# Two transformer blocks on one core: modulation sums in PSUM tiles of their own, another order of work in the opening, and the memory's projections placed differently

## The chip, the core and the metric

The kernel runs on one core of a Trainium2 chip. The metric is the device time of one execution in microseconds (us), from the median of several executions; less is better. Engine names are those of the profile: PE (TensorE, matrix products; PEld are its weight loads), DVE (VectorE), ACT (ScalarE), POOL (GpSimd), SP (SyncE, which here only issues DMAs). SPq and ACTq are the instructions with which SP and ACT issue DMAs. All arithmetic is in 32-bit floats; most products are made of a high and a low part of each operand, so that one logical product is three matmuls (high by high, high by low, low by high).

## The reference, cut to what matters

```python
# first block (x: 512 x 1024, c: 1024)
mod = silu(c) @ w_ada + b_ada                      # 3072 wide
shift, scale, gate = split(mod, 3)
h = rms_norm(x, g_pre) * (1 + scale) + shift
proj = h @ w_in                                    # q, k, v, forget gate, gates, for two attentions
...                                                # forgetting attention and sliding-window attention
x = x + gate * rms_norm(concat(oa, ob) @ w_out, g_post)
# second block (mem: 256 x 1024)
h = rms_norm_2(x, norm_g)
mem_h = rms_norm_2(mem, mem_norm_g)
...                                                # convolution, differential attention
k, v = split(mem_h @ w_mem_kv, 2)                  # 1024 columns of keys, 1024 of values
k = rms_norm_2(k.reshape(M, 4 heads, 256), kn_g)
...                                                # cross attention to the memory, gated sum, w_out
```

## The kernel before

The program is one long list of tiles and operations. An engine executes its instructions in the order in which they stand. That order is written out by hand in the opening (the engines are wrapped there in `Ordered`, whose helper is line 345, so that nearly all of the opening carries the line L345 in a profile). After the opening a scheduler sets the order from its own estimate of durations. PSUM has four pools: `mm` (three banks), `sc` (two), `tp` (two), `pv` (one). A new tile of a pool takes over the bank of the tile that many places earlier and has to wait until that one's readers are done. A tile is tracked as a whole: a write waits for earlier reads of any column of it.

**Opening, about 0 to 105 us.** SP loads the memory `mt`, the first 512 columns of the memory's weights `rawm`, the input `xn`, and the modulation weights `ada` in eight chunks of 1 MB through five buffers; chunk k yields 128 columns of shift and 128 of scale. Memory's transpose `mT` and its first key half `kb_` are made on PE. `squares` (ACT) sums the squares of x, `rsqrt_small` is ten short DVE steps, then x is scaled (two quarters on DVE, two on ACT) and `x_transpose` turns it with PE and copies it out with ACT into `xt`. The modulation sums of chunks 0, 1, 3, 4 and 6 are made by `products` (two products on ACT, six on DVE and an add) followed by `sums` (a matmul with one column of ones); those of chunks 2, 5 and 7 by `sums_pe` (matmuls with one column each). All eight write columns of one tile, `pm`. `modulate(k)` (DVE) turns two columns of `pm` into shift and scale, `hidden(k, ...)` makes the high part `hh` (ACT) and low part `hl` of the modulated input. Then come the products with `w1c` (keys, values and forget gates of the second attention; four banks `wb`, one of them of the pool `mm`), whose weights are split into `wh` (ACT cast) and `wl` (subtraction on DVE or POOL) by `load_w`; `on_pool` names the pieces that POOL gets. Weight loads use three buffers `raw`. The queries `qb` follow (96 matmuls of line L221, banks of `mm`), then the first gate `zb0` (line L202).

**Middle, about 315 to 410 us.** The first block's output product `w_out` runs in two halves of 256 rows (`hf`), each in two column halves (`cp`) of 48 matmuls. After each half comes a chain of DVE and ACT steps: a norm, the residual `yg`, its squares (ACT L961), a second norm, `hn` (DVE L924). PE transposes `hn` later, in `finish`. In between, `mem_p(i)` makes a quarter of the memory's keys and values from the stored `mT`: 48 matmuls into two `sc` banks, which ACT then copies out as `mv` (L905). Quarter 0 is the `kb_` of the opening, quarter 1 the second key half, 2 and 3 the values.

```python
for i in ((1, 2), (3,))[hf]:
    run(mem_p(i, sc_tile))
```

Of the kernel before, what the change touches and what calls it, by code (L numbers as in the profile page):

```python
# [15 lines left out]
ALU = mybir.AluOpType  # L16
# [4 lines left out]
P = 128  # L21
S = 512
NT = 4
KT = 8
# [68 lines left out]
def two_block_kernel(ctx: ExitStack, tc: tile.TileContext, A: dict, out: bass.AP):  # L93
    nc = tc.nc
    pe, act, dve, pool = nc.tensor, nc.scalar, nc.vector, nc.gpsimd
# [18 lines left out]
    def V(name, i=None):  # L114
        a, b = VEC[name]
        return vec[:, a:b] if i is None else vec[:, a + i:a + i + 1]
# [5 lines left out]
    ident, ones = C("ident"), C("ones")  # L122
# [6 lines left out]
    def f(ap):  # L129
        return ap.bitcast(F32)  # L130
# [15 lines left out]
    def mm_tile():  # L146
        return psm.tile([P, 512], F32, tag="mm", name="mm")
# [4 lines left out]
    def tp_tile():  # L152
        return pst.tile([P, 512], F32, tag="tp", name="tp")
# [176 lines left out]
    cs = const.tile([P, 8], F32, name="cs")  # L330
# [33 lines left out]
    with ExitStack() as st:  # L364
# [9 lines left out]
        mod = pa1.tile([P, 16], F32, name="mod")  # L374
        free = (pe, act, dve, pool)
        pe, act, dve, pool, sp = (Ordered(e) for e in free + (nc.sync,))
# [16 lines left out]
        def squares(x, ss, ts):  # L393
            for t in ts:
                act.activation(out=xt[:, 2 * t:2 * t + 2, :].rearrange("p a b -> p (a b)"), in_=x[:, t, :], func=AF.Square, accum_out=ss[:, t:t + 1])
# [13 lines left out]
                    dve.scalar_tensor_tensor(out=d[i % 2], in0=a[:, i, :], scalar=cs[:, i:i + 1], in1=d[i % 2], op0=ALU.mult, op1=ALU.add)  # L409
                dve.tensor_tensor(out=d[0], in0=d[0], in1=d[1], op=ALU.add)  # L410

        pm = tp_tile()

        def sums(k):
            for j in range(2):
                pe.matmul(out=pm[:, 2 * k + j:2 * k + j + 1], lhsT=accs[k][0][:, j * P:(j + 1) * P], rhs=ones[:, 0:1], start=True, stop=True)

        def sums_pe(k):
            for j in range(2):
                for i in range(KT):  # L420
                    pe.matmul(out=pm[:, 2 * k + j:2 * k + j + 1], lhsT=adas[k][:, i, j * P:(j + 1) * P], rhs=cs[:, i:i + 1], start=(i == 0), stop=(i == KT - 1))

        def modulate(k):
            c_ = slice(2 * k, 2 * k + 2)
            dve.scalar_tensor_tensor(out=mod[:, c_], in0=pm[:, c_], scalar=0.5, in1=V("b_ada")[:, c_], op0=ALU.mult, op1=ALU.add)
            dve.scalar_tensor_tensor(out=gs[:, k:k + 1], in0=mod[:, 2 * k + 1:2 * k + 2], scalar=1.0, in1=V("g_pre", k), op0=ALU.add, op1=ALU.mult)

        def hidden(k, by, eng):
# [34 lines left out]
        xss = pa.tile([P, NT], F32, tag="xss", name="xss", bufs=1)  # L463
        squares(mt, mss, range(2))
        dve.tensor_copy(out=mrs, in_=rsqrt_small(pa, mss, 2, 1.0 / 1024, 1e-6, "rn2"))
        squares(xn, xss, range(NT))
        r = rsqrt_small(pa, xss, NT, 1.0 / 1024, 1e-6, "rn4")
        products(0, act)
        for t in range(2):
            dve.tensor_scalar(out=xn[:, t, :], in0=xn[:, t, :], scalar1=r[:, t:t + 1], scalar2=None, op0=ALU.mult)  # L470
            act.activation(out=xn[:, t + 2, :], in_=xn[:, t + 2, :], func=AF.Copy, scale=r[:, t + 2:t + 3])
        products(0, dve)
        products(1, act)
        products(1, dve)
        x_transpose(range(KT))
        sums(0)
        sums_pe(2)
        load_ada(5, 6, 7)
        sums(1)
        products(3, act)  # L480
        modulate(0)
        hidden(0, dve, pool)
        for t in range(2):
            act.activation(out=mk[:, t, :], in_=kb_[t], func=AF.Copy, scale=mrs[:, t:t + 1])
        products(3, dve)
        modulate(1)
        hidden(1, dve, pool)
        products(4, act)
        products(4, dve)
        modulate(2)  # L490
        hidden(2, dve, pool)
        sums_pe(5)
        sums(3)
        sums_pe(7)
        sums(4)
        products(6, act)
        modulate(5)
        hidden(5, act, pool)
        modulate(3)
        hidden(3, act, pool)  # L500
        w = load_w(A["w1c"], 264, on_pool=(1, 3), queue=sp)
        sp.dma_start(out=mT_d, in_=mT)
        products(6, dve)
        modulate(7)
        hidden(7, act, pool)
# [386 lines left out]
    def mem_p(i, bank):  # L892

        if not MV:
            mh, ml = (mvp.tile([P, KT, 256], F32R, name=n) for n in ("mh", "ml"))
            nc.sync.dma_start(out=f(ml), in_=mT_d)
            act.copy(out=mh, in_=f(ml))
            pool.tensor_tensor(out=ml, in0=f(ml), in1=f(mh), op=ALU.subtract)
            MV[0] = (mh, ml)
        w = load_w(A["w_mem"][i], NW)  # L900
        banks = [bank() for t in range(2)]
        yield from mm_W(banks, w, *MV[0], range(2))
        mv = mvp.tile([P, 2, NW], F32, tag="mv", name="mv", bufs=2)
        for t in range(2):
            act.activation(out=mv[:, t, :], in_=banks[t], func=AF.Copy, scale=mrs[:, t:t + 1])  # L905
        if i == 1:
            mem_k_norm(mvp, mv, 1)
        else:
            nc.scalar.dma_start(out=v_d[:, :, (i - 2) * NW:(i - 1) * NW], in_=mv)
        yield  # L910

    with ExitStack() as st:
        yp = open_pool(st, "yp", reuse_waits="tile")
        yk = open_pool(st, "yk", 2, reuse_waits="tile")
        ngb = yp.tile([P, 1024], F32, name="ngb")
        nc.scalar.dma_start(out=ngb, in_=A["rows"][:, 2048:3072])
        later = []

        def finish(i):
            hf, yg, rs = later[i]  # L920
            for t in range(2):
                tk = 2 * hf + t
                hn = yk.tile([P, 1024], F32, tag="hn", name="hn")
                dve.scalar_tensor_tensor(out=hn, in0=yg[t], scalar=rs[t], in1=ngb, op0=ALU.mult, op1=ALU.mult)  # L924
                for kq in range(2):
                    ps = tp_tile()
                    for k in range(4):
                        pe.transpose(out=ps[:, k * P:(k + 1) * P], in_=hn[:, (4 * kq + k) * P:(4 * kq + k + 1) * P], identity=ident)
                    pv_ = ps.rearrange("p (k q) -> p k q", k=4)
                    d = (slice(None), slice(4 * kq, 4 * kq + 4), slice(tk * P, (tk + 1) * P))  # L930
                    act.copy(out=hh[d], in_=pv_)
                    dve.tensor_tensor(out=hl[d], in0=pv_, in1=f(hh[d]), op=ALU.subtract)

        for hf in range(2):
            xs = [yk.tile([P, 1024], F32, tag=f"xs{t}", name="xs", bufs=1) for t in range(2)]
            yg = [yk.tile([P, 1024], F32, tag=f"yg{t}", name="yg") for t in range(2)]
            ss = yk.tile([P, 2, 2], F32, tag="yss", name="yss")
            s2 = yk.tile([P, 2], F32, tag="ys2", name="ys2")
            for t in range(2):
                nc.scalar.dma_start(out=xs[t], in_=A["xn"][2 * hf + t])  # L940
            for cp in range(2):
                pt_ = [mm_tile() for t in range(2)]
                ws = load_w(A["w_out"][cp], NW, order=(2, 3, 0, 1) if hf + cp == 0 else None)
                if hf and cp == FINCP:
                    finish(0)
                run(mm_W(pt_, ws, oh, ol, (2 * hf, 2 * hf + 1), order=oorder if hf + cp == 0 else range(KT)))
                for t in range(2):
                    q = yk.tile([P, S], F32, tag="yq", name="yq")
                    cs_ = slice(cp * 512, (cp + 1) * 512)
                    act.activation(out=q, in_=pt_[t], func=AF.Square, accum_out=ss[:, t, cp:cp + 1])  # L950
                    dve.tensor_tensor(out=yg[t][:, cs_], in0=pt_[t], in1=ggb[:, cs_], op=ALU.mult)
            s3 = yk.tile([P, 2], F32, tag="ys3", name="ys3")
            rs = []
            for g in ((0,), (1,)) if hf in TOKW else ((0, 1),):
                gs_, n = slice(g[0], g[-1] + 1), len(g)
                dve.tensor_tensor(out=s2[:, gs_], in0=ss[:, gs_, 0], in1=ss[:, gs_, 1], op=ALU.add)
                r = rsqrt_small(yk, s2[:, gs_], n, 1.0 / 1024, 1e-6, f"yr{n}")
                for i, t in enumerate(g):
                    dve.scalar_tensor_tensor(out=yg[t], in0=yg[t], scalar=r[:, i:i + 1], in1=xs[t], op0=ALU.mult, op1=ALU.add)
                    q = yk.tile([P, 1024], F32, tag="yq2", name="yq2", bufs=1)  # L960
                    act.activation(out=q, in_=yg[t], func=AF.Square, accum_out=s3[:, t:t + 1])  # L961
                    nc.scalar.dma_start(out=x1_d[2 * hf + t], in_=yg[t])
                r = rsqrt_small(yk, s3[:, gs_], n, 1.0 / 1024, 1e-6, f"yr2{n}")
                rs += [r[:, i:i + 1] for i in range(n)]
            later.append((hf, yg, rs))
            for i in ((1, 2), (3,))[hf]:
                run(mem_p(i, sc_tile))
            if hf:
                finish(1)
# [593 lines left out]
```

## Time and profile before

| | us |
|---|---|
| median of 3 runs | 1209.71 (1207.82 to 1210.49) |
| the profiled execution | 1206.4 |
| its span, first to last instruction | 1204.6 |
| PE busy | 1153.9 (96 %), mean granted clock 0.979 |
| DVE, ACT, POOL busy | 880.2 (73 %), 566.1 (47 %), 206.7 (17 %) |

The rows of the section further down come from the profiled execution. Its own time is 1.8 us above its span. A busy share is an average over all stages; the time when a stage is short of something is seen in waits and in stretches.

### The profile page before, as it was taken

What the parts mean: (1) busy time and instruction counts of PE and PEld (TensorE: products, weight loads), DVE (VectorE), ACT (ScalarE), POOL (GpSimd) and SP (SyncE); (2) the same over time, 40 slices, a digit from 0 to 9 for tenths busy, and PEclk for the clock granted to TensorE, in tenths of its full rate; (3) what the DMA queues carried; (4) which work ended last, traced back from release to release, by engine and by line L of the source; (5) the groups of instructions that cost most, each with busy time, mean ns of one, the idle gap of its engine ahead of it and who ended that gap; (6) DMA issues with size and microseconds to landing.
All of it is one profiled execution on the core that took longest, in us unless ns stands there. A gap on an engine that the chain in (4) does not pass through costs nothing.

```text
span 1204.6 us, 16398 instructions
## 1 busy us (share of the span) xinstructions
PE 1153.9 (96%) x5668; PEld 954.6 (79%) x5668; DVE 880.2 (73%) x1877; ACT 566.1 (47%) x1260; POOL 206.7 (17%) x157
## 2 busy tenths in 40 slices
PE   7689999999889999999999989999999999999998
PEld 5677877777668888888888878888888888888887
DVE  5368876558677679999999998998876377453342
ACT  6165665537556436454554544454433235242221
POOL 0144000100222221203012131122101131110100
PEclk9589999999989999999999999999999999999999
DMA  9254312543376442333333433434468446423333
GB/s 377 118 199 130 98 57 64 165 143 106 111 261 216 155 115 88 100 104 96 104 106 114 123 105 132 132 106 135 142 225 293 133 155 210 150 88 94 98 105 105
DMA packets 59330, 167.36 MB, mean 139 GB/s; under 512 B 7056, under 2 KB 10384, under 8 KB 57968
## 3 DMA queue, kind: packets, MB, share of 16 engines
q1 hardware_dynamic: 36112, 124.50, 32.9%
q10 hardware_dynamic: 23136, 41.81, 10.0%
q8 instruction: 45, 0.74, 0.3%
q14 instruction: 37, 0.30, 0.1%
HBM read 137.85 MB, written 21.63 MB: 132 GB/s over the span
## 4 chain that ended last, share of the span: by engine, by line
PE 72%; DVE 19%; DMA 3%; issue 3%; ACT 2%; POOL 1%; SPq 0%; ACTq 0%; DVEq 0%; POOLq 0%
PE mm L202 40%; PE mm L221 15%; DVE cv L1010 5%; DVE wl L172 3%; PE sc L221 2%; PE tp L345 2%; PE mm L213 1%; DVE dp L1122 1%; PE sc L345 1%; PE pv L856 1%; PE mm L792 1%; DMA raw<-in_w_mem_dram 1%; PE sc L1274 1%; PE pv L1317 1%; DVE acc L345 1%
## 5 line engine op out<-in xcount | busy, mean ns | idle before, releaser
L170 ACT CAST wh<-raw 128x512 fp32r<-128x512 f32 x360 | 217.6, 620 | 217.1 <-PE mm L202 114.6
L172 DVE TENSOR_TENSOR wl<-raw,wh 128x512 fp32r<-128x512 f32 x270 | 203.1, 764 | 101.2 <-ACT wh L170 98.8
L172 POOL TENSOR_TENSOR wl<-raw,wh 128x512 fp32r<-128x512 f32 x90 | 129.6, 1440 | 824.4 <-ACT wh L170 760.6
L202 PE MATMUL mm<-hh,wh 128*128 128x512 f32 x640 | 253.7, 396 | 0.0
L202 PE MATMUL mm<-hl,wh 128*128 128x512 f32 x640 | 251.9, 394 | 0.0
L202 PE MATMUL mm<-hh,wl 128*128 128x512 f32 x640 | 251.8, 394 | 0.0
L1010 DVE SCALAR_TENSOR_TENSOR cv<-u,vec,cv 128x512 f32<-128x512 f32 x240 | 192.5, 802 | 2.1
L202 PEld LDWEIGHTS mm<-hh,wl 128*128 128x128 f32 x640 | 120.7, 189 | 24.8 <-issue 0.2
L202 PEld LDWEIGHTS mm<-hh,wh 128*128 128x128 f32 x640 | 120.7, 189 | 24.1 <-issue 0.5
L202 PEld LDWEIGHTS mm<-hl,wh 128*128 128x128 f32 x640 | 120.7, 189 | 23.3 <-issue 0.2
L221 PE MATMUL mm<-wl,hh 128*128 128x512 f32 x256 | 100.9, 394 | 0.0
L221 PE MATMUL mm<-wh,hh 128*128 128x512 f32 x256 | 100.9, 397 | 0.0
L221 PE MATMUL mm<-wh,hl 128*128 128x512 f32 x256 | 100.5, 394 | 0.0
L202 PE MATMUL mm<-bh,wh 128*128 128x512 f32 x192 | 75.3, 392 | 0.0
L202 PE MATMUL mm<-bh,wl 128*128 128x512 f32 x192 | 74.8, 390 | 0.0
L202 PE MATMUL mm<-bl,wh 128*128 128x512 f32 x192 | 74.8, 389 | 0.0
L1124 ACT ACTIVATE dp<-dp,dst 128x128 f32<-128x128 f32 (+3 forms) x64 | 35.8, 559 | 50.9 <-DVE dst L1122 49.6
L221 PEld LDWEIGHTS mm<-wh,hl 128*128 128x128 f32 x256 | 48.2, 188 | 9.6
L221 PEld LDWEIGHTS mm<-wh,hh 128*128 128x128 f32 x256 | 48.2, 188 | 9.0
L221 PEld LDWEIGHTS mm<-wl,hh 128*128 128x128 f32 x256 | 48.2, 188 | 8.5
L202 PEld LDWEIGHTS mm<-bl,wh 128*128 128x128 f32 x192 | 36.1, 188 | 7.7 <-issue 0.2
L202 PEld LDWEIGHTS mm<-bh,wh 128*128 128x128 f32 x192 | 36.1, 188 | 7.7 <-issue 0.2
(375 smaller groups left out, 2157.0 us busy)
## 6 DMA issues: line engine op xcount, KB each, us to landing
raw<-in_w_dram SPq DMA_DIRECT2D x88, 512.0 KB, 4.1
raw<-in_w_out_dram SPq DMA_DIRECT2D x24, 512.0 KB, 4.3
raw<-in_w2n_dram SPq DMA_DIRECT2D x24, 512.0 KB, 4.0
ada<-in_w_ada_dram SPq DMA_DIRECT2D x8, 1024.0 KB, 5.5
raw<-in_w_mem_dram SPq DMA_DIRECT2D x12, 512.0 KB, 3.7
raw<-in_w1n_dram SPq DMA_DIRECT2D x8, 512.0 KB, 5.9
wg<-in_w_gate_dram SPq DMA_DIRECT2D x8, 512.0 KB, 4.8
k<-ks SPq DMA_DIRECT2D x32, 128.0 KB, 3.7
```

Of the source, the lines that this page charges most:

```text
L170: act.copy(out=wh, in_=raw[:, s])
L172: eng.tensor_tensor(out=wl, in0=raw[:, s], in1=f(wh), op=ALU.subtract)
L202: m = pe.matmul(out=ps, lhsT=a[:, c0:c0 + P], rhs=at(b, k), start=(n == 0 and i == 0), stop=(n == KT - 1 and i == 2))
L213: pe.matmul(out=ps, lhsT=at(a, k)[:, t * P:(t + 1) * P], rhs=b[:, 0:n], start=(start and m == 0 and i == 0), stop=(stop and m == len(order ...
L221: x = pe.matmul(out=ps, lhsT=at(a, k)[:, t * P:(t + 1) * P], rhs=b[:, 0:n], start=(m == 0 and i == 0), stop=(m == KT - 1 and i == 2))
L345: return lambda *a, **k: tc.keep_in_program_order(fn(*a, **k))
L792: m = pe.matmul(out=pm, lhsT=csb[:, 2 * q + k, :], rhs=a[:, k, :], start=(q + k == 0), stop=(2 * q + k == KT - 1))
L856: pe.matmul(out=pv[0:64, j * P:], lhsT=l_, rhs=r_[:, j, j * P:], start=(j == 0 and i == 0), stop=(j == NT - 1 and i == 2))
L1010: dve.scalar_tensor_tensor(out=a, in0=u[:, j:j + S], scalar=dw[:, m * 31 + j:m * 31 + j + 1], in1=a, op0=ALU.mult, op1=ALU.add)
L1122: dve.tensor_tensor_reduce(out=p_[:, :w], in0=ps[:, :w], in1=wb[:, S - w:], scale=1.0, scalar=FMAX, op0=ALU.add, op1=ALU.min, accum_out=st ...
L1124: act.activation(out=p_[:, :w], in_=p_[:, :w], func=AF.Exp, scale=-1.0, bias=st_[:, 0, n, m:m + 1], accum_out=st_[:, 1, n, m:m + 1])
L1274: pe.matmul(out=ps[:, t * 256:(t + 1) * 256], lhsT=a[:, k, n * P:(n + 1) * P], rhs=b[:, k, :], start=(cnt == 0), stop=(cnt == 5))
```

## The change

Each chunk's sums get a tile of their own (`pms[k]`): chunks 0, 1, 7 and 4 in the pool `tp`, chunks 2, 5, 3 and 6 in the pool `mm`. The hand-written order of the opening is changed. `products(0, ...)` stands ahead of the squares of x, `products(3, ...)` ahead of `modulate(0)`, and `hidden(1)` ahead of the copies of `kb_`; `products(6, act)` stands behind the casts of `w1c`, whose subtractions go to DVE but for two pieces. In `mem_p` the split of the memory into `mh` and `ml` is made in four pieces, the subtraction on DVE in place of POOL. Quarter 1 of the memory moves from the first half of rows to the second.

```diff
-        pm = tp_tile()
+        pms = {}
 
         def sums(k):
+            pms[k] = tp_tile() if k in (0, 1, 7, 4) else mm_tile()
             for j in range(2):
-                pe.matmul(out=pm[:, 2 * k + j:2 * k + j + 1], lhsT=accs[k][0][:, j * P:(j + 1) * P], rhs=ones[:, 0:1], start=True, stop=True)
+                pe.matmul(out=pms[k][:, j:j + 1], lhsT=accs[k][0][:, j * P:(j + 1) * P], rhs=ones[:, 0:1], start=True, stop=True)
...
         def modulate(k):
             c_ = slice(2 * k, 2 * k + 2)
-            dve.scalar_tensor_tensor(out=mod[:, c_], in0=pm[:, c_], scalar=0.5, in1=V("b_ada")[:, c_], op0=ALU.mult, op1=ALU.add)
+            dve.scalar_tensor_tensor(out=mod[:, c_], in0=pms[k][:, 0:2], scalar=0.5, in1=V("b_ada")[:, c_], op0=ALU.mult, op1=ALU.add)
...
         dve.tensor_copy(out=mrs, in_=rsqrt_small(pa, mss, 2, 1.0 / 1024, 1e-6, "rn2"))
+        products(0, act)
+        products(0, dve)
         squares(xn, xss, range(NT))
         r = rsqrt_small(pa, xss, NT, 1.0 / 1024, 1e-6, "rn4")
-        products(0, act)
...
         sums(0)
+        sums(1)
+        products(3, act)
+        products(3, dve)
         sums_pe(2)
         load_ada(5, 6, 7)
-        sums(1)
-        products(3, act)
         modulate(0)
         hidden(0, dve, pool)
+        modulate(1)
+        hidden(1, dve, pool)
         for t in range(2):
             act.activation(out=mk[:, t, :], in_=kb_[t], func=AF.Copy, scale=mrs[:, t:t + 1])
-        products(3, dve)
-        modulate(1)
-        hidden(1, dve, pool)
+        modulate(2)
+        hidden(2, dve, pool)
         products(4, act)
         products(4, dve)
-        modulate(2)
-        hidden(2, dve, pool)
         sums_pe(5)
         sums(3)
         sums_pe(7)
         sums(4)
-        products(6, act)
...
-        w = load_w(A["w1c"], 264, on_pool=(1, 3), queue=sp)
+        w = load_w(A["w1c"], 264, queue=sp)
         sp.dma_start(out=mT_d, in_=mT)
+        products(6, act)
         products(6, dve)
...
-            act.copy(out=mh, in_=f(ml))
-            pool.tensor_tensor(out=ml, in0=f(ml), in1=f(mh), op=ALU.subtract)
+            for k in range(0, KT, 2):
+                d = slice(k, k + 2)
+                act.copy(out=mh[:, d], in_=f(ml[:, d]))
+                dve.tensor_tensor(out=ml[:, d], in0=f(ml[:, d]), in1=f(mh[:, d]), op=ALU.subtract)
...
-            for i in ((1, 2), (3,))[hf]:
+            for i in ((2,), (1, 3))[hf]:
                 run(mem_p(i, sc_tile))
```

The change also moves instructions. On ACT, early in the opening: `acc<-ada,cs` are the two products of a chunk, `xt,xss<-xn` the squares of x (which use `xt` as scratch), `xt<-mm` the copies of the transposed x.

```order
+L541 ACTIVATE cn<-rn,halfpi 128x128
+L345 ACTIVATE acc<-ada,cs 128x256 x2
 L345 ACTIVATE xt,xss<-xn 128x1024 x4
-L345 ACTIVATE acc<-ada,cs 128x256 x2
 L345 ACTIVATE xn<-xn,ry 128x1024 x2
 L345 ACTIVATE acc<-ada,cs 128x256 x2
 L345 COPY xt<-mm 128x512 x8
```

The products of chunk 0 have moved ahead of the four squares of x.

On PE, from the transposes of x to the last sums ahead of `w1c`: `128x1` are the one-column matmuls, `cst,acc` those of `sums`, `cs,ada` those of `sums_pe`.

```order
 L345 MATMUL mm<-cst,xn 128x128 x32
-L345 MATMUL tp<-cst,acc 128x1 x2
-L345 MATMUL tp<-cs,ada 128x1 x16
-L345 MATMUL tp<-cst,acc 128x1 x2
-L345 MATMUL tp<-cs,ada 128x1 x16
-L345 MATMUL tp<-cst,acc 128x1 x2
+L345 MATMUL tp<-cst,acc 128x1 x4
+L345 MATMUL mm<-cs,ada 128x1 x32
+L345 MATMUL mm<-cst,acc 128x1 x2
 L345 MATMUL tp<-cs,ada 128x1 x16
 L345 MATMUL tp<-cst,acc 128x1 x2
```

The count is the same; chunk 1 now stands ahead of chunk 2, and the sums of chunks 2, 5 and 3 have moved into banks of the pool `mm`. A little further on, PE had 28 matmuls of `qb` between those of `w1c`; in the changed program all 96 stand behind the last one of `w1c`.

On ACT, in the second half of rows, the changed program from the copies of the last `w_out` bank (`yq<-mm`) to the first copies of a memory quarter (`mv`):

```order
L954 ACTIVATE yq,yss<-mm 128x512 x2
L170 CAST wh<-raw 128x512 x6
L965 ACTIVATE yq_3707,ys_3690<-yg 128x1024
L966 DMA x_d<-yg 128x1024
L170 CAST wh<-raw 128x512
L965 ACTIVATE yq_3711,ys_3690<-yg 128x1024
L966 DMA x_d<-yg 128x1024
L170 CAST wh<-raw 128x512
L909 ACTIVATE mv<-sc,mrs 128x512 x2
```

The same rows stood there before (L950, L961 and L905 then); `mv` was the copy of quarter 3, the last. Now it is that of quarter 1, and quarter 3's matmuls follow into the same two banks.

## Rows read from the trace of the kernel before

**Rows 1.** Waits of PE: who for whom, us in total, times, longest.

```profile
PE tp L345 <- DVE mod L345: 11.5, 2, 10.2
PE sc L221 <- ACT mv L905: 5.7, 1, 5.7
PE sc L345 <- ACT wh L345: 4.1, 1, 4.1
```

**Rows 2.** The chain that ended last, 0 to 110 us: start us, us, what.

```profile
7.02 3.40 PE mm L345 x15
...
24.16 3.73 PE mm L345 x32
27.89 5.66 PE tp L345 x40
...
43.77 15.53 PE tp L345 x72
...
77.17 0.36 PE pv L345 x3
...
97.17 2.25 PE tp L669 x8
99.42 0.59 PE tp L295 x4
...
105.60 0.93 PE mm L202 x4
```

**Rows 3.** Timeline of ACT, opening: start us, us, instruction, count, idle before.

```profile
14.93 1.04 ACT L345 ACTIVATE xt<-xn 128x1024 f32<-128x1024 f32 x1
...
20.21 0.91 ACT L345 ACTIVATE acc<-ada,cs 128x256 f32<-128x256 f32 x2 [1.03 <-DMA ada<-in_w_ada_dram]
21.26 2.19 ACT L345 ACTIVATE xn<-xn,ry 128x1024 f32<-128x1024 f32 x2
...
62.94 1.96 ACT L345 CAST wh<-raw 128x264 fp32r<-128x264 f32 x6
```

**Rows 4.** Timeline of DVE, opening.

```profile
19.21 0.17 DVE L345 TENSOR_SCALAR rv<-xss 128x4 f32<-128x4 f32 x1 [4.01 <-ACT xt L345]
...
21.20 1.42 DVE L345 TENSOR_SCALAR xn<-xn,ry 128x1024 f32<-128x1024 f32 x2
...
80.65 0.69 DVE L345 TENSOR_TENSOR hl<-ht,hh 128x512 fp32r<-128x512 f32 x1
```

**Rows 5.** PE by stretches: us, busy (count), granted clock, DMA share, GB/s.

```profile
24.00:28.00 4.00, 4.00 (x37) 1.00 1.01 428
...
30.00:31.00 1.00, 1.00 (x10) 0.86 1.02 426
...
44.00:59.00 15.00, 15.00 (x72) 0.50 0.00 0
65.00:68.00 3.00, 3.00 (x15) 0.50 0.62 167
68.00:70.00 2.00, 2.00 (x17) 0.93 1.09 385
...
345.00:348.00 3.00, 2.97 (x7) 0.50 0.96 330
```

**Rows 6.** The chain that ended last, 300 to 420 us.

```profile
345.03 12.62 PE sc L221 x48
357.64 10.88 PE mm L221 x48
...
381.21 10.88 PE sc L221 x48
```

**Rows 7.** Timeline of ACT, 295 to 415 us.

```profile
344.31 1.24 ACT L905 ACTIVATE mv<-sc,mrs 128x512 f32<-128x512 f32 x2
...
392.98 1.26 ACT L905 ACTIVATE mv<-sc,mrs 128x512 f32<-128x512 f32 x2
```

**Rows 8.** Timeline of POOL, 315 to 330 us.

```profile
322.40 4.63 POOL L898 TENSOR_TENSOR ml<-ml,mh 128x2048 fp32r<-128x2048 f32 x1 [0.52 <-ACT mh L897]
```

More of the change, by code (lines that the diff above doesn't have):

```diff
@@ L410, in products @@
                 dve.tensor_tensor(out=d[0], in0=d[0], in1=d[1], op=ALU.add)
-        pm = tp_tile()
+        pms = {}
         def sums(k):
+            pms[k] = tp_tile() if k in (0, 1, 7, 4) else mm_tile()
             for j in range(2):
-                pe.matmul(out=pm[:, 2 * k + j:2 * k + j + 1], lhsT=accs[k][0][:, j * P:(j + 1) * P], rhs=ones[:, 0:1], start=True, stop=True)
+                pe.matmul(out=pms[k][:, j:j + 1], lhsT=accs[k][0][:, j * P:(j + 1) * P], rhs=ones[:, 0:1], start=True, stop=True)
         def sums_pe(k):
+            pms[k] = tp_tile() if k in (0, 1, 7, 4) else mm_tile()
             for j in range(2):
                 for i in range(KT):
-                    pe.matmul(out=pm[:, 2 * k + j:2 * k + j + 1], lhsT=adas[k][:, i, j * P:(j + 1) * P], rhs=cs[:, i:i + 1], start=(i == 0), stop=(i == KT - 1))
+                    pe.matmul(out=pms[k][:, j:j + 1], lhsT=adas[k][:, i, j * P:(j + 1) * P], rhs=cs[:, i:i + 1], start=(i == 0), stop=(i == KT - 1))
         def modulate(k):
             c_ = slice(2 * k, 2 * k + 2)
-            dve.scalar_tensor_tensor(out=mod[:, c_], in0=pm[:, c_], scalar=0.5, in1=V("b_ada")[:, c_], op0=ALU.mult, op1=ALU.add)
+            dve.scalar_tensor_tensor(out=mod[:, c_], in0=pms[k][:, 0:2], scalar=0.5, in1=V("b_ada")[:, c_], op0=ALU.mult, op1=ALU.add)
             dve.scalar_tensor_tensor(out=gs[:, k:k + 1], in0=mod[:, 2 * k + 1:2 * k + 2], scalar=1.0, in1=V("g_pre", k), op0=ALU.add, op1=ALU.mult)
@@ L471, in two_block_kernel @@
             act.activation(out=xn[:, t + 2, :], in_=xn[:, t + 2, :], func=AF.Copy, scale=r[:, t + 2:t + 3])
-        products(0, dve)
         products(1, act)
```

## The prediction

> **What bounds the kernel now.** PE is busy for 96 % of the span, so I read first what it waits for in the rest. Two waits stand out [rows 1]. One of 10.2 us is on a `modulate` of DVE, in the opening; one of 5.7 us is on the copies `mv` of a memory quarter. The chain that ended last shows both in place. In the opening it is with PE from 24.16 to 33.55 us (transposes of x, then forty one-column matmuls), leaves it until 43.77, comes back for 72 more to 59.30, and the first gate `zb0` begins at 105.60 [rows 2]. The hole is the tile `pm`: chunk 5's sums may not write it before chunk 2's columns are read, and that reading stands on DVE behind two chunks of products. The middle is seen in the chain of 300 to 420 us [rows 6]. Third, PE's clock by stretches [rows 5]: after the transposes it falls to the lower level (0.50 of 2.4 GHz) at 30 to 31 us, although PE is recorded as busy with one-column matmuls; fifteen further microseconds of these leave it there; it comes back only at about 68 us, some 3.3 us into the dense products with `w1c`. From `zb0` on I count on PE as the bound, so what `zb0` gains the end gains.
>
> **The head of the opening gets later.** ACT runs in order. The products of chunk 0 waited for their load and began at 20.21, after the squares of x [rows 3]. Now the squares stand behind them: they start at 20.21 + 0.91 = 21.1 instead of 14.93, so the reading of their sums at 19.21 [rows 4] becomes 25.4, DVE's small norm takes 21.20 - 19.21 = 2.0 as before [rows 4], ACT's scaling 2.19 [rows 3], and x is scaled at 29.6. Before, that was 23.45 and hidden: the transposes began at 24.16, when the memory's key products left PE. So their start moves by 5.5 us, with PE idle.
>
> **What that does to PE's clock** no row of this place shows. After the wait of 5.7 us in the middle PE restarted at 345 at the lower level [rows 1, 5, 6], so I let the 32 transposes begin there. Their pace is 3.73 / 32 = 0.117 us at full level; the memory's transposes at 7.02 ran at 3.40 / 15 = 0.227 [rows 2], which I take for the lower one, since the one-column matmuls show the same ratio below. Bounds: none raises the clock, 32 x 0.227 = 7.3 us; or it rises after 3.3 us as at 65 to 68.3 us [rows 5], 14 at 0.227 and 18 at 0.117, 5.4 us. I take 5.4, end at 35.0: with the full level held over 24 to 28 us by transposes alone, they count as work here [rows 5].
>
> The Trainium skill says otherwise, in "TensorE: Matmul & The Clock Gate", Part 4: a transpose does not count as busy for the clock gate, so a stretch of them would not bring the full clock. The granted clock of 1.00 over 24 to 28 us speaks against it, but that is a case of holding, not of rising; by the page it would be the slow case, the first rival.
>
> **The sums.** Forty took 5.66 us from 27.89, of which 3.0 at full level up to about 30.9; 72 took 15.53 at the lower, 0.216 each [rows 2, 5]. So (5.66 - 3.0) / 0.216 = 12 were slow and 28 ran in the first 3.0 us, 0.11 each. The same 112 now follow without the hole: 28 in 3.0 us, 84 x 0.216 = 18.1, end at 35.0 + 21.1 = 56.1 instead of 59.30. Chunk 5's sums are the 72nd: 35.0 + 3.0 + 44 x 0.216 = 47.5, and `modulate(5)` follows at once, since DVE's products of chunk 4 are done by then (chunk 2's sums end near 40.5, and I put 5 us for the products).
>
> **`w1c`.** Before, its casts began at 62.94 [rows 3], 3.6 us after the last sums at 59.30, which both chunks 5 and 3 waited for. Now 47.5 + 3.6 = 51.1, with the weights long there. The last hidden chunk, 6, had its low part at 80.65 + 0.69 = 81.3 [rows 4], 18.4 us after the casts began: fourth load, products of chunk 6, `modulate(7)`, `(4)`, `(6)`. The steps between are the same; DVE's two additional subtractions and POOL's two fewer lie beside the wait for the fourth load. So chunk 6 is ready at 69.5. PE, in order, begins `w1c` at 56.1: 15 matmuls at the lower clock until 59.4, 33 at 0.36 / 3 = 0.12 [rows 2] until 63.4, chunk 6's sums, three more chunks of 12, 68.2. There it waits 1.3 us for chunk 6 and ends at 69.5 + 1.4 = 70.9.
>
> **`qb` pays something back.** Its second bank now is the one that the last `wb` tile had, so it waits for a copy on ACT and an add on DVE behind `w1c`'s end; from the short steps there I put 0.7 us (bounds 0 and 2). 28 of its 96 matmuls no longer fill `w1c`'s waits. All 96 follow: 96 x 10.88 / 48 = 21.8 us [rows 6], then 2.25 + 0.59 for the sums of the forget gates and four transposes [rows 2]. `zb0` starts at 70.9 + 0.7 + 21.8 + 2.8 = 96.2 instead of 105.60: **9.4 us gained**.
>
> **Memory.** Quarter 2's matmuls needed quarter 1's banks. They began at 345.03, after the copy that began at 344.31 [rows 6, 7]; the wait was 5.7 us [rows 1], and the slow clock made the 48 take 12.62 instead of 10.88, 1.7 more [rows 6]. Now `w_out`'s next half, in other banks, follows quarter 2; its weights take the places in the load queue that quarter 2's had. That gives 7.4 us. But quarters 1 and 3 now follow each other in the second half, into the same two banks. There the only quarter began at 381.21 and its copy at 392.98, 11.8 later [rows 6, 7], with the same six casts, square, cast, square, cast ahead of it on ACT. The next matmuls can start 0.7 behind a copy's start, at 12.5; PE is through with quarter 1 at 10.9. A wait of 1.6 us is left; bounds 0 and the whole old 7.4. Net **5.8 us**. Behind it waits nothing: `hn` for the last transposes comes from the same DVE steps, ahead of quarter 3's end. POOL's subtraction of 4.63 us [rows 8] goes to DVE in four pieces (0.69 for one of this shape [rows 4]: 2.8 us); quarter 1, the first product with the memory, ended 5.7 ahead of 345.03 and took some 10.9, so it began near 328.4, 1.4 us after POOL was done at 327.03, and now `w_out`'s products stand in its place and the memory's come a quarter later, so they cost nothing; without that cover it would be their 2.8 us. Moving them also frees the POOL piece of the weights behind.
>
> **Sum.** 9.4 + 5.8 = 15.2 us. The profiled execution took 1206.4, of which 1204.6 is span; it would take 1191.2. The median of the runs is 3.3 above it, so 1209.7 - 15.2 = 1194.5.
>
> **Rivals.**
> *The clock stays low through the transposes.* They end at 29.6 + 7.3 = 36.9; 112 x 0.216 = 24.2 gives 61.1 for the sums and 36.9 + 72 x 0.216 = 52.5 for chunk 5. Casts at 56.1, chunk 6 at 74.5, `w1c`'s end at 75.9, `zb0` at 101.2: 4.4 us gained there, 10.2 in all, 1199.5. For it: one-column matmuls did not raise the clock in 15 us. Against it: transposes held it.
> *The memory's wait only moves.* If the second half's chain were as late as the first's was (quarter 2's start lay 5.7 behind quarter 1's end, and the clock fell), the memory part gives 0 and the whole is 9.4: 1200.3. For it: the order on ACT ahead of `mv` is the same in both. Against it: the rows of the second half have 11.8, not 16.
> *Slower: the chunk loads starve.* Chunk 7's load needs the buffer that `sums_pe(2)` releases, now at about 35.0 + 3.0 + 12 x 0.216 = 40.6 instead of 33.55 - 4 x 0.216 = 32.7, and `w1c`'s loads stand behind it on SP. Its 1 MB takes 2.5 us at 428 GB/s [rows 5]; doubled for its latency, an estimate, it is there at 45.6, 2.8 before PE comes to it at 47.5 + 4 x 0.216 = 48.4. Each microsecond beyond that goes to the end; no gain is left from 2.8 + 15.2 = 18 us of lateness, and it is slower by over 0.2 % (2.4 us, about what a measurement here can tell) from 20.4. The DMA engines stood idle from 44 to 59 before [rows 5], so hardly.
>
> **How the numbers follow.** Forecast 0.55 (1191 to 1198), low clock 0.22 (1197 to 1202), moved wait 0.12 (1198 to 1203), both together 0.04 (4.4 in all, 1205.3), a gain beyond 19 us 0.03, no difference or slower 0.04. Range 1190 to 1202. Faster by over 0.2 %: 0.94; within: 0.03; slower: 0.03.
>
> **What would show it.** Right: ACT's products of chunk 0 still at about 20.2 with the squares behind; PE idle from 24.2 to about 29.6; no wait of the sums on `modulate`; casts of `w1c` near 51, `zb0` near 96; no wait behind the first half's memory quarter and one of 1 to 3 us between quarters 1 and 3. Wrong: transposes of x at 0.227 to the end; a wait of `w1c` or `qb` on weights; the quarters' wait above 5 us; or a later stage in which PE waits for something that does not move with `zb0`.

## The result, and the profile after

The changed kernel took 1195.01 us in the median of four executions (1191.20 to 1195.66), the kernel before 1209.99 (four, 1207.82 to 1210.49): a ratio of 0.9873, 95 % interval 0.9849 to 0.9897, 15.0 us less where 15.2 were forecast (the table ahead of the prediction has the median of the first three executions of the kernel before). The two profiled executions lie only 10.7 us apart: 1206.4, which is 3.6 below the median of its kernel, and 1195.66, which is 0.7 above. That gap of 4.2 us between the two ways of comparing turned out to be no property of the change; it is taken up with the first experiment.

Waits of PE in the changed kernel (who for whom, us in total, times, longest):

```profile
PE mm L345 <- DVE xn L345: 3.9, 1, 3.9
PE sc L221 <- ACT mv L909: 3.2, 1, 3.2
```

The two waits of [rows 1] that the forecast spoke of, 10.2 and 5.7 us, are replaced by these: PE now waits for the scaled x, and for the copy of quarter 1 of the memory.

The chain that ended last, opening, changed kernel (start us, us, what):

```profile
27.03 2.20 ACT xn L345 x2
...
29.27 5.73 PE mm L345 x29
35.01 0.79 PE tp L345 x8
35.79 12.79 PE mm L345 x68
48.58 7.68 PE tp L345 x36
...
71.02 21.81 PE mm L221 x96
...
95.66 13.64 PE mm L202 x60
```

Against [rows 2]: the 112 records of one-column matmuls (the program has 56 of these, and the profile lists each twice) run from 35.01 to 56.26 without a hole, `w1c` ends at 71.02, `qb` follows at once, `zb0` starts at 95.66 instead of 105.60. Two timelines give the steps on the other engines. ACT, changed kernel (start us, us, instruction, count, idle before):

```profile
19.89 0.91 ACT L345 ACTIVATE acc<-ada,cs 128x256 f32<-128x256 f32 x2 [5.25 <-DMA ada<-in_w_ada_dram]
20.70 1.04 ACT L345 ACTIVATE xt<-xn 128x1024 f32<-128x1024 f32 x1
...
51.05 1.96 ACT L345 CAST wh<-raw 128x264 fp32r<-128x264 f32 x6
```

DVE, changed kernel:

```profile
24.98 0.17 DVE L345 TENSOR_SCALAR rv<-xss 128x4 f32<-128x4 f32 x1 [1.62 <-ACT xt L345]
...
46.85 0.42 DVE L345 TENSOR_TENSOR acc<-acc 128x256 f32<-128x256 f32 x1
47.77 0.16 DVE L345 SCALAR_TENSOR_TENSOR mod<-mm,vec 128x2 f32<-128x2 f32 x1 [0.49 <-PE mm L345]
...
68.80 0.69 DVE L345 TENSOR_TENSOR hl<-ht,hh 128x512 fp32r<-128x512 f32 x1 [0.23 <-ACT hh L345]
```

The squares of x stand behind chunk 0's products, 5.8 us later than in [rows 3]; the norm of x begins at 24.98 instead of 19.21 [rows 4]. `modulate(5)` runs at 47.77, half a microsecond behind the end of VectorE's products of chunk 4 (46.85 + 0.42). The first casts of `w1c` are at 51.05 instead of 62.94.

PE by stretches, changed kernel (us, busy and count of PE, PEld, DVE, ACT, POOL, then PE's granted clock, DMA share, GB/s):

```profile
28.00:34.00 6.00, 5.74 (x25) 5.04 (x26) 3.28 (x8) 4.83 (x9) 0.00 (x0) 0.50 0.70 259
34.00:36.00 2.00, 2.00 (x21) 2.00 (x19) 0.00 (x0) 1.95 (x5) 0.00 (x0) 0.97 0.93 393
36.00:38.00 2.00, 2.00 (x19) 2.00 (x18) 1.88 (x5) 0.48 (x2) 0.00 (x0) 0.89 0.18 70
38.00:60.00 22.00, 22.00 (x103) 22.00 (x104) 15.20 (x35) 10.61 (x21) 8.41 (x7) 0.50 0.47 168
```

After the idle time the transposes start at the lower level (1.2 GHz) and reach the full one (2.4 GHz) at 34 us, among the last of them; the one-column matmuls fall back to 0.50 by 38 us and stay there although PE is recorded as fully busy.

The chain of the middle, changed kernel:

```profile
309.44 12.10 PE mm L221 x45
321.54 10.88 PE sc L221 x48
332.42 10.88 PE mm L221 x48
...
369.77 0.59 ACT mv L909
...
370.41 11.18 PE sc L221 x48
```

Quarter 2 of the memory (321.54) is followed at once by `w_out`'s second column half; no wait of 5.7 us and no slow 12.62 us behind it as in [rows 6]. Quarter 3 starts at 370.41 with the copy of quarter 1 just ahead of it, after a wait of 3.2 us.

### The profile page after: what moved, and what is told of

Same layout as the page of the kernel before. It is cut to its first block, busy times and chain, and to the rows that moved or that the text cites. A ratio compares the mean times of both kernels' runs of the same rounds, so it can differ in the third digit from the quotient of the medians.

```text
span 1193.9 us, 16406 instructions
## 1 busy us (share of the span) xinstructions
PE 1158.9 (97%) x5668; PEld 958.5 (80%) x5668; DVE 876.6 (73%) x1883; ACT 566.4 (47%) x1263; POOL 197.1 (17%) x154
## 4 chain that ended last, share of the span: by engine, by line
PE 76%; DVE 15%; DMA 3%; ACT 2%; issue 2%; POOL 0%; ACTq 0%; SPq 0%; DVEq 0%
PE mm L202 42%; PE mm L221 16%; DVE cv L1014 4%; PE mm L213 2%; DVE wl L172 2%; PE mm L345 2%; PE sc L221 2%; DVE dp L1126 1%; PE pv L858 1%; PE sc L1278 1%; PE pv L1321 1%; PE mm L794 1%; DMA ada<-in_w_ada_dram 1%; PE tp L295 1%; DMA k<-ks 1%
## 5 line engine op out<-in xcount | busy, mean ns | idle before, releaser
L172 DVE TENSOR_TENSOR wl<-raw,wh 128x512 fp32r<-128x512 f32 x270 | 194.5, 732 | 100.2 <-ACT wh L170 98.6
L172 POOL TENSOR_TENSOR wl<-raw,wh 128x512 fp32r<-128x512 f32 x90 | 126.9, 1410 | 830.2 <-ACT wh L170 798.7
```

The costliest lines, as they stand in the source:

```text
L172: eng.tensor_tensor(out=wl, in0=raw[:, s], in1=f(wh), op=ALU.subtract)
```

## The experiments

They ran in three groups of four; the kernel before took 1207.69, 1207.59 and 1206.52 us in them. Ratios are to that.

**The changed kernel once more (e5), and its two parts alone (e1, e2).** In e1 the memory's split and the places of its quarters are as before; in e2 the opening is:

```diff
 e1, against the changed kernel
-            for k in range(0, KT, 2):
...
+            act.copy(out=mh, in_=f(ml))
+            pool.tensor_tensor(out=ml, in0=f(ml), in1=f(mh), op=ALU.subtract)
-            for i in ((2,), (1, 3))[hf]:
+            for i in ((1, 2), (3,))[hf]:
 e2, against the kernel before: these lines the other way round
```

> The changed kernel once more, unaltered, as the measure for the others on this chip. If the two parts add up and differences between executions come from dips of PE's clock: 10.5 (opening alone) + 5.7 (memory alone) = 16.2 below the kernel before, so 1191.5 where that takes 1207.7, and executions that spread over 4 us. If the memory part is worth only the 1 us by which the two profiled executions differed beyond the opening's 9.9: 1197.

> The opening as in the changed kernel, the memory's split and the places of its quarters as before. By the forecast's terms the opening gives 9.4 us (zb0 at 96.2; the profile of the changed kernel had it at 95.66, so 9.9): 1210.0 - 9.4 to 9.9 = 1200.1 to 1200.6, and the wait of 5.7 us behind quarter 1 is there again. Rival: the opening's gain is partly given back later, since the profile of the changed kernel shows the granted clock falling at 188 and at 304 us where before it did not (some 3 us): 1203 to 1204.

> The opening as before, the memory's split in pieces and its quarters placed as in the changed kernel. By the forecast's terms 5.8 us: 1204.2, with a wait of 1.6 to 3.2 us between quarters 1 and 3. Rival: the two profiled executions lie only 10.7 us apart, of which the opening takes 9.9, so the memory's part is worth 1 us at most: 1209.

e5: 1192.39, ratio 0.9874 (0.9857 to 0.9890), 15.2 us. e1: 1197.20, ratio 0.9914 (0.9897 to 0.9931), 10.5 us. e2: 1201.97, ratio 0.9952 (0.9938 to 0.9967), 5.7 us. The parts add up to 16.2. The rival of e2, which put the memory part at 1 us, falls, and so does that of e1, by which some 3 us of the opening's gain would be given back later. e1 has the wait on `mv` again (5.6 us); e2 has 2.5 between quarters 1 and 3.

Then why were the two profiled executions only 10.7 us apart? Because the same program meets dips of PE's clock at different places. PE by stretches, the profiled execution of the changed kernel (1195.66 us):

```profile
184.00:192.00 8.00, 6.22 (x19) 4.34 (x20) 4.52 (x16) 2.75 (x9) 0.00 (x0) 0.79 0.53 167
300.00:308.00 8.00, 5.64 (x29) 3.73 (x26) 2.41 (x5) 2.65 (x6) 0.00 (x0) 0.79 0.00 0
308.00:316.00 8.00, 6.57 (x22) 5.25 (x23) 4.49 (x6) 4.47 (x11) 1.29 (x1) 0.79 0.56 197
364.00:372.00 8.00, 4.83 (x22) 3.68 (x21) 7.26 (x20) 6.03 (x13) 0.48 (x1) 1.00 0.85 295
700.00:712.00 12.00, 9.91 (x43) 8.01 (x42) 10.14 (x31) 5.53 (x17) 3.68 (x3) 0.86 0.38 131
```

The same five stretches in e5's profiled execution, the same program (1191.35 us):

```profile
184.00:192.00 8.00, 6.50 (x31) 5.07 (x30) 4.42 (x18) 3.34 (x11) 0.00 (x0) 1.00 0.49 156
300.00:308.00 8.00, 5.00 (x21) 3.34 (x20) 2.63 (x4) 2.05 (x4) 0.00 (x0) 0.79 0.12 21
308.00:316.00 8.00, 8.00 (x37) 6.64 (x36) 6.39 (x9) 6.56 (x15) 2.71 (x2) 1.00 0.66 241
364.00:372.00 8.00, 6.28 (x20) 5.00 (x21) 7.09 (x22) 4.70 (x14) 1.28 (x1) 0.79 0.70 237
700.00:712.00 12.00, 9.88 (x47) 7.92 (x46) 9.94 (x31) 6.59 (x19) 3.06 (x3) 1.00 0.38 118
```

Each stretch of 8 us at 0.79 lacks 8 x 0.21 = 1.7 us of full clock, an estimate of what it can cost at most. The first execution has three of these and 12 x 0.14 = 1.7 more at 700: 6.7; e5 has two: 3.4. The 3.3 between them, and a clock in the transposes that rose 2 us earlier in e5 (`zb0` at 94.12), make up about the 4.3 us by which the two differ. (Here and below a start of `zb0` in an experiment is the timeline's, which puts it at 95.42 in the first profile and at 105.35 in the kernel before.) The kernel before had two such dips in its profile, 0.79 from 316 to 324 us and 0.83 from 714 to 724, 3.4 us like e5, and a third that belongs to the wait on `mv` and goes with it.

**The late head undone (e3).**

```diff
-        products(0, act)
-        products(0, dve)
         squares(xn, xss, range(NT))
         r = rsqrt_small(pa, xss, NT, 1.0 / 1024, 1e-6, "rn4")
+        products(0, act)
         for t in range(2):
...
+        products(0, dve)
         products(1, act)
```

> The changed kernel with the products of chunk 0 back behind the squares of x on ACT and behind the scaling of x on DVE. If the late head is what it cost: ACT's products still at 20, x scaled at 23.4, transposes of x from 24.2 to 27.9 at the full clock, sums over at 27.9 + 3.0 + 18.1 = 49.0, 7 us earlier than 56.1, and all behind it: 1195.0 - 7 = 1188. Rival: the loads or VectorE's products of chunks 3 and 4 then set the start of the w1c casts, and 3 us or less are left: 1192 to 1195.

1186.98, ratio 0.9827 (0.9808 to 0.9846): 5.4 us below e5, where 7 were expected and the rival had 3 or less. PE's timeline in e3:

```profile
24.37 3.89 PE L345 MATMUL mm<-cst,xn 128*128 128x128 f32 x32
28.10 1.00 PE L345 MATMUL tp<-cst,acc 128*128 128x1 f32 x8
...
47.97 0.99 PE L345 MATMUL tp<-cst,acc 128*128 128x1 f32 x4
48.82 0.57 PE L345 MATMUL sc<-wh,hh 128*128 128x264 f32 x1
```

The transposes are back where they were before, at the full clock, and `w1c` starts at 48.8; `zb0` is at 88.22, 7.2 earlier than in the changed kernel's profile and 5.9 earlier than in e5's. So the head's lateness, which the forecast counted, is real time, and it was avoidable: ACT's products start when their load lands, at 20.1 here and 19.9 there, whether the squares stand ahead of them or behind.

**The tile and the order apart (e7, e8).** e7 is the kernel before with only the sums' tiles changed (`pms[k]`); e8 is the changed kernel with one tile `pm` again.

```diff
 e7, against the kernel before
-        pm = tp_tile()
+        pms = {}
...
+            pms[k] = tp_tile() if k in (0, 1, 7, 4) else mm_tile()
 e8, against the changed kernel: the same, the other way round
```

> The kernel before with nothing changed but the sums: a tile for each chunk. By the forecast's reading the shared tile made the hole of 10.2 us: it goes, sums end at 33.55 + 72 x 0.216 = 49.1, modulate(5) follows modulate(2) on VectorE at about 45, the casts begin near 49, and with 39.4 us of PE work between sums and zb0 (56.26 to 95.66 in the changed kernel) zb0 starts at 88.5 to 91.4, 14 to 17 earlier than 105.6: 1191 to 1194, better than the whole opening of the change. Rival: VectorE's order is the cause (modulate(2) behind two chunks of products), and without moving it the wait goes on to modulate(5) and the casts: zb0 at 100 or later, 1202 or more.

> The changed kernel with all sums in one tile again, the order left as changed. If the order alone did it: PE waits under 1 us, the time stays within 1 us of the changed kernel. If the tile is needed too, because modulate(5) then waits for the last sums written to it: casts at 56.1 + 3.6 = 59.7 instead of 51.05, a wait of about 4 us of PE on them, zb0 at 105.6 - (62.94 - 59.7) = 102.4, 6.7 us later than with tiles of their own: 6 to 7 us above the changed kernel.

e7: 1188.44, ratio 0.9833 (0.9817 to 0.9850), 19.2 us below the kernel before, and 4 below the whole change, though its memory part is the old one. Its `zb0` begins at 86.85, a little earlier still than the 88.5 to 91.4 worked out. PE's timeline in e7:

```profile
28.21 4.21 PE L345 MATMUL mm<-cs,ada 128*128 128x1 f32 x32
32.28 0.99 PE L345 MATMUL tp<-cst,acc 128*128 128x1 f32 x4
33.50 6.96 PE L345 MATMUL mm<-cs,ada 128*128 128x1 f32 x32 [0.23 <-DMA ada<-in_w_ada_dram]
...
48.00 0.99 PE L345 MATMUL tp<-cst,acc 128*128 128x1 f32 x4
```

ACT's timeline in e7:

```profile
44.98 1.96 ACT L345 CAST wh<-raw 128x264 fp32r<-128x264 f32 x6
```

Chunk 5's sums follow at 33.50, held for 0.23 us by their load alone. The gain is larger than the hole: the sums end some 10 us earlier than before (48.9 instead of 59.3), but the casts of `w1c` begin 18.0 earlier (44.98 instead of 62.94 in [rows 3]), and `zb0` comes 18.5 earlier. e8: 1202.14, ratio 0.9955 (0.9936 to 0.9973), 9.8 us above e5; 6 to 7 had been worked out. Its rows show both sides of a shared tile, PE first, then DVE:

```profile
40.68 6.99 PE L345 MATMUL tp<-cs,ada 128*128 128x1 f32 x32 [1.94 <-DVE mod L345]
...
59.97 0.59 PE L345 MATMUL sc<-wh,hh 128*128 128x264 f32 x1 [3.77 <-ACT wh L345]
```

```profile
56.23 0.16 DVE L345 SCALAR_TENSOR_TENSOR mod<-tp,vec 128x2 f32<-128x2 f32 x1 [9.14 <-PE tp L345]
```

The write waits for the earlier read (1.94), and the read of chunk 5 waits for the last write of a chunk that it does not need: `modulate(5)` at 56.23 instead of 47.77, and the casts behind it. With the new order and one tile, the medians show no gain of the opening: 1202.14 is 0.2 us above e2, where only the memory part is changed. In its profile `zb0` does start earlier, at 102.1 against 107.3 in e2 and 105.35 in the kernel before; e8's executions spread over 6.6 us, and by the two intervals a gain of some 3 us is not excluded.

**Quarter 3 in other banks (e4), and with the head undone (e6).**

```diff
-                run(mem_p(i, sc_tile))
+                run(mem_p(i, mm_tile if i == 3 else sc_tile))
```

> The changed kernel with quarter 3 of the memory in banks of the pool mm, so that it does not wait for the copies of quarter 1. If that wait is real time on the path, its 3.2 us go (no wait, and no slower clock behind it): 1195.0 - 3.2 = 1191.8. Rival: the wait only moves, to the banks of mm that the last w_out products left (released by the same queue on ACT) or to the transposes in finish: 1195.

> The changed kernel with the squares of x first again and quarter 3 in banks of mm. If both gains stand on different stretches of PE's path they add: 1187.0 - 3.2 = 1183.8. If either had been a matter of the clock's chance (e3's profiled execution had one dip less than others), 1187.

e4: 1190.26, ratio 0.9855 (0.9840 to 0.9870), 2.1 below e5; its slowest execution (1190.36) lies below e5's fastest (1191.33). e6: 1183.85, ratio 0.9798 (0.9782 to 0.9813), 3.1 below e3, and so at the 1183.8 that the sum gave. Part of the wait only moved. PE in e4, the product behind quarter 3, in the bank that quarter 3 had:

```profile
379.86 0.50 PE L221 MATMUL mm<-wh,hh 128*128 128x512 f32 x1 [1.32 <-ACT mv L909]
```

So of e4's two theories neither holds whole: 3.2 us of wait became 1.3 at the next place.

**The memory's split on POOL (e11),** e4 with the one-piece split of the kernel before:

> The kernel of e4 (changed, with quarter 3 in mm) with the memory's split in one piece and its subtraction on POOL again. By the forecast the split costs and gives nothing where quarter 1 no longer follows at once: within 1 us of e4's 1190.3. Rival: the pieces of the weights behind it on POOL come late, as before at 320 us, and w_out or the next quarter waits: 2 to 5 us more.

1193.82, ratio 0.9887 (0.9869 to 0.9906): 3.6 us above e4, and no execution of the one lies among those of the other. The rival holds. (The engine and the number of pieces change together here; which of the two it takes is not separated.) POOL in e4, then in e11:

```profile
314.51 1.85 POOL L172 TENSOR_TENSOR wl<-raw,wh 128x512 fp32r<-128x512 f32 x1 [2.86 <-ACT wh L170]
320.02 1.29 POOL L172 TENSOR_TENSOR wl<-raw,wh 128x512 fp32r<-128x512 f32 x1 [3.66 <-ACT wh L170]
```

```profile
312.12 4.62 POOL L900 TENSOR_TENSOR ml<-ml,mh 128x2048 fp32r<-128x2048 f32 x1 [0.51 <-ACT mh L899]
316.69 1.74 POOL L172 TENSOR_TENSOR wl<-raw,wh 128x512 fp32r<-128x512 f32 x1
323.94 1.29 POOL L172 TENSOR_TENSOR wl<-raw,wh 128x512 fp32r<-128x512 f32 x1 [5.51 <-ACT wh L170]
```

POOL's weight pieces come 2.2 and then 3.9 us later. DVE's first weight piece in e4, then in e11:

```profile
313.93 0.68 DVE L172 TENSOR_TENSOR wl<-raw,wh 128x512 fp32r<-128x512 f32 x1
```

```profile
312.59 4.69 DVE L172 TENSOR_TENSOR wl<-raw,wh 128x512 fp32r<-128x512 f32 x1 [2.13 <-ACT wh L170]
```

The delay goes by way of DVE, too, and not only of POOL's own queue. DVE's subtraction of one weight piece took 4.69 us beside POOL's long one, where it took 0.68 with POOL idle. In all four kernels with the split on POOL (before, e1, e7, e11) the DVE piece that started beside it took 3.6 to 4.7 us and ended 0.5 to 0.6 us behind POOL's end. DVE's first five pieces are done at 318.1 in e4, although DVE makes the memory's split ahead of them, and at 320.8 in e11. The next loads into the buffers `raw` wait for these pieces: from 295 to 330 us SP's longest wait for one is 7.0 us in the four kernels, and 4.3 to 4.9 in the changed kernel, e2 to e5, e8 and e9. ACT then waits 4.78 us for the next weights of the memory in e11 (0.79 in e4) and casts them at 322.72 instead of 318.80, and POOL's second late piece stands on that cast. Then PE is reached: in e11 it waits 1.07 us at 342.85 for a cast of `w_out`'s weights, where e4 waits for none, and 3.3 behind quarter 3 where e4 waits 1.3; the clock dips behind that (0.63 from 384 to 388 us, 1.00 in e4).

**All parts that paid (e9):** e7 with the memory part of the change and quarter 3 in `mm`.

> The kernel before with a tile for each chunk's sums (its order of the opening kept), the memory's split and quarters as in the changed kernel, and quarter 3 in banks of mm. If the parts add: 1207.6 - 19.2 (tiles alone) - 5.7 (memory alone) - 1 to 2 (what the other banks bring when the wait partly moves to the next product in mm) = 1181 to 1182. Rival: with the opening 19 us earlier the loads of the middle are late and the memory's gain is lost: 1187.

1180.62, ratio 0.9781 (0.9761 to 0.9800), 25.9 us below the kernel before, close to the 1181 to 1182 by which the parts add up, and the lowest median of all. It keeps the order of the opening as it was. Against e6, which has the new order behind an early head, the intervals overlap, so whether the rest of the new order costs or not stays open.

**Wider sums (e10, e12):** e6 and e9 with every matmul of the sums 64 columns wide, all alike.

```diff
-                pe.matmul(out=pms[k][:, j:j + 1], ..., rhs=ones[:, 0:1], ...)
+                pe.matmul(out=pms[k][:, j * W1:(j + 1) * W1], ..., rhs=ones[:, 0:1].to_broadcast([P, W1]), ...)
```

> The kernel of e6 (squares first, quarter 3 in mm) with every matmul of the sums 64 columns wide instead of one, all columns alike. If one-column matmuls count too little for the clock: it stays at the full level after the transposes, 112 matmuls at 0.11 to 0.13 each take 12.3 to 14.6 instead of 20, w1c starts at the full clock too: 7 to 9 us less, 1175 to 1177, unless the load of chunk 5 or 7 (33 us and later) holds them. If the clock falls whatever their width: 1183.9, or up to 5 more if 64 columns take longer at the lower level.

> The kernel of e9 with the sums 64 columns wide. Here chunk 5's load lands at 33.4 and already held the sums by 0.2 us in e7, and chunk 7's buffer is free only when chunk 2's sums end. If the clock stays full: sums bounded by chunk 7's load, some 5 us after 31.5, then 16 more at 0.12: end at 40 to 43 instead of 49, and the casts of w1c and VectorE's products set the rest: 3 to 8 us less than e9. If the clock falls whatever the width: as e9.

e10: 1185.08, ratio 0.9820 (0.9800 to 0.9840); e12: 1183.24, ratio 0.9800 (0.9775 to 0.9825). No gain over e6 and e9 by the medians, where 7 to 9 and 3 to 8 us were expected. (In e12's profile `zb0` starts at 86.2, 1.9 ahead of e9's; the intervals of the two overlap.) PE by stretches, e10:

```profile
30.00:38.00 8.00, 7.89 (x71) 7.75 (x70) 7.04 (x17) 5.05 (x10) 2.79 (x2) 1.00 0.88 336
38.00:40.00 2.00, 1.04 (x10) 1.07 (x10) 2.00 (x3) 0.23 (x1) 1.44 (x1) 1.00 1.00 383
40.00:42.00 2.00, 2.00 (x13) 2.00 (x12) 1.93 (x8) 0.00 (x0) 0.00 (x0) 0.55 0.09 33
42.00:50.00 8.00, 7.29 (x33) 6.99 (x33) 3.52 (x8) 4.80 (x10) 3.44 (x3) 0.50 0.17 39
```

The clock did stay full longer, until behind a wait for chunk 7's load at 38 to 39 us, and the sums ended at 45.5 instead of 48.7. But `modulate(5)` stood at 41.71 (41.05 in e6): it follows VectorE's products of chunk 4 there, not PE, and with it the casts (44.98 and 44.33). What the sums gained, PE waited in `w1c`: 0.71 us at 46.78 for a weight piece and 1.72 at 56.06 for `modulate`. In e12 the wait for chunk 5's load grew to 1.1 us at 33.5, and the clock fell behind it (0.63 from 34 to 36 us).

## Why the prediction was right, point by point

**The hole.** Right, and e7 shows it alone: the shared tile made the 10.2 us. The forecast named the tile only for the write that waits. That the reads of chunks 5 and 3 waited for the last sums stands in its sum for the casts, but without the tile as the reason; e8 showed that the tile made this half too, and in e7 the casts of [rows 3] come 18.0 us earlier with it gone.

**The head.** Right: squares from 20.70 (21.1 forecast), norm at 24.98 (25.4), the rest of x scaled at 29.2 (29.6). e3 prices it at 5.4 us.

**The clock in the transposes.** The end came at 35.01 where 35.0 was forecast, and that closeness is luck, since the way there was different: the full level came only at 34, not 3.3 us after the start, and three transposes of the quarters that DVE had scaled went ahead at 27.87. In e5, same program, the level was back at 32 to 34 us (0.96), and `zb0` was 1.3 us earlier; the term is uncertain by about that. The pace of 0.227 us at the lower level was read from the memory's transposes at 7.02, for which the profile lists a clock of 1.00 (the trace holds no record of the clock before 10.2 us); the figure holds all the same, as 16 transposes from 30.61 took 3.62 us at 0.50. In both executions the level rose while PE ran nothing but transposes. The Trainium skill, "TensorE: Matmul & The Clock Gate", Part 4, says that a transpose does not count as busy for the clock gate; these traces differ from it, here in raising the level (in e5 0.50 at 30 to 32 us and 0.96 at 32 to 34, under transposes alone) as before in holding it (1.00 over 24 to 28 us). The rows call them MATMUL against the identity and do not tell whether the transpose mode that the page speaks of is on.

**Sums and `w1c`.** Sums end 56.26 (56.1), casts 51.05 (51.1), chunk 6's low part 68.80 + 0.69 = 69.5 (69.5), end of `w1c` 71.02 (70.9). One step was wrong without harm: the clock came back between 60 and 62 us, not at 59.4, so the products ahead of chunk 6 ran later, and the 1.3 us that PE was to wait for chunk 6 went into that. And VectorE was no 2 us ahead of PE at chunk 5, but half a microsecond; a faster PE gains nothing there (e10).

**`qb`.** 0.7 us were put on the second bank, and it cost nothing: all 96 follow `w1c` in one piece, 71.02 to 92.83. That makes the opening 9.9 instead of 9.4 in the profile, 10.5 by the medians of e1.

**Memory.** The net was right (5.8 forecast, 5.7 in e2), its parts were not, so that the net came out is luck. The wait between quarters 1 and 3 is 2.5 to 3.2 us in e2, e3, e5 and the first profile, not 1.6. And the move of the split from POOL was put at nothing, with the first product with the memory named as its cover; the forecast saw that POOL's next weight piece comes free, and gave that no time. e11 prices the split at 3.6 us, beside e4. If that price holds where the quarters stand as before, it leaves about 2 us of the 5.7 for their new places, where the forecast gave them all of it. What the forecast missed is that POOL's subtraction of 4.63 us [rows 8] held up DVE's weight pieces beside it, and by them the loads. The kernel before shows the same signs (a DVE piece of 3.90 us at 323.67, SP's wait of 7.0 us, a cast at 333.15 that waits 3.81 us for its load). Whether its wait of 5.7 us came from that was not tried (the split alone in the kernel before would tell).

**The sum** is then 10.5 + 5.7 = 16.2 by parts and 15.2 in e5. That the first profile showed only 10.7 less is, for the most part, the dips of the clock; that one pair of profiles would have led to a wrong finding about the memory part.

## What to carry to other kernels

Before reordering engines around a tile that many steps write and read by columns, give each step a tile of its own, leave the order alone at first, and measure: here that edit alone gave 19.2 us, and the new order with it took 8.8 of them back (e1 against e7). Ask of a step that is moved ahead what it starts on: chunk 0's products began when their load landed, and all that had been free to run before them now stood behind them. An instruction that is hidden in itself can still hold its engine's queue; price it by who is next on that engine and by what runs beside it on the others, not by when its own result is wanted.

## What the hardware showed that was not expected

A subtraction on VectorE that started beside a long one on GpSimd did not end before it: 4.69 us instead of 0.68 in e11, 3.90 in the kernel before, each ending some 0.5 us behind GpSimd's end.

Executions of one program differ by some microseconds: e8's by 6.6, the changed kernel's by 4.5, e4's by only 0.3. In the two profiles of the changed kernel most of the difference comes from short falls of PE's clock, and the same wait did not always bring one. Behind a wait of 1.5 us (at 187.49 and at 186.12) the stretch of 184 to 192 us had a granted clock of 0.79 in one execution and 1.00 in the other, with almost the same PE busy time; behind waits of 3.2 and 3.1 us the stretch of 364 to 372 had 1.00 and 0.79.

Under matmuls 64 columns wide the granted clock of e10 was 1.00 from 30 to 40 us; under one-column matmuls that of e6 was 0.68 at 32 to 34 us and 0.50 from 34 on. After its fall in e10, behind a wait of 1.06 us, it was 0.50 to 0.55 from 40 to 50 us, under the last of the wide matmuls and the first of `w1c`.
